# A hybrid decoder step: other transfer times in the order model, and norms spread by a product of 128 rows

## The chip, the cores and the metric

The kernel runs on one core of one Trainium2 chip, in one launch. A time is the device time of that core in microseconds (us). Three executions of the kernel before took 1326.87, 1324.06 and 1327.06 us; their median, 1326.87, is the time before. The profiled execution is a fourth one: 1324.27 us, of which 1322.5 lie between its first and its last instruction (its span).

## The reference, cut to what matters

One layer is computed for 1024 prompt steps and 8 x 8 sample steps, 1088 columns in all, with a model width of 1024:

```
h = rmsnorm(x, g_mix_in)
gate_a, x_a, q, k, v, z_c, xbc, dt_raw = split(h @ w_in)
out_a = rg_lru(conv4(x_a)) * gelu(gate_a)                     # width 256
out_b = three dilated window branches of attention on q, k, v # 6 heads x 64, sample steps with a cache
out_c = rmsnorm(ssd(silu(conv4(xbc)), dt, A) * silu(z_c))     # 6 heads x 64, chunks of 128 steps
x = x + rmsnorm(concat(out_a, out_b, out_c) @ w_out)
x = x + rmsnorm((silu(g) * u) @ w_down)   with  g, u = split(rmsnorm(x) @ w_gate_up)   # width 2816
```

Everything is float32.

## The kernel before, in words

Columns are steps (`T` = 1088), in three groups of 364, 362 and 362 (`GROUPS`). Rows are channels, in tiles of 128. A float32 product is made of three products of rounded parts (`mm3`: high weights by high x, high by low, low by high), so that each weight tile is loaded as float32 from memory, rounded (`round`, on VectorE or ScalarE, whichever the order model finds less loaded) and subtracted (`rest`, on VectorE).

The work has four stretches. First the input is scaled and multiplied by the first two tiles of `w_in`. From about 100 to 640 us TensorE makes the other projections and, from about 415 us, the products of `w_out` (both called main products here; they stand in bank0 and bank6, later in more banks) and between them the three mixers: the chunked scan of mixer C to about 220 us, attention to about 497 us, and then the norms after `w_out`. From 640 to 1220 us it makes the gate, up and down products, and at the end the last tiles and the final norm.

The order of all this is not written out. The generators (`scan`, `unit`, `norm_c`, `out_norm`, `projections` and so on) yield conditions, and class `Flow` keeps a clock of its own, `now`, and a guess for when each engine is free and each piece of memory is written. `Flow.run` takes the first task whose condition holds by that guess; `step` picks for each of the other engines the ready instruction of the lowest rank. What comes out is the order in which instructions are put on each engine, and nothing more: on the chip each engine works through its own list in order, and waits at an instruction whose inputs are not there, with everything behind it. For a transfer on SyncE `step` guesses `QUEUE` for its issue, then `FLIGHT`, then a time by its bytes and `RATE`, one transfer after the other, and then `RECEIPT` until its data count as landed (lines 142, 271 to 274 and 319). `RATE` is in bytes per us.

`inverse_norm` (line 567) turns a sum of squares over 128 partitions into one factor per column, the same on all partitions. A product with ones sums the partitions (128x1, three of them), POOL takes the power, the factors are split into high and low parts, a transpose puts them into 6 rows, VectorE spreads them over a tile `spread` (`t7` in the order) of 6 rows by up to 364 columns with zeros where they don't belong, and one last product, of 6 rows of ones by that tile, puts the factors on all 128 partitions. This runs 14 times: three times for the input, three for mixer C's norm, six after `w_out`, two at the end.

In `chunk` the state `S` of the scan is multiplied by the chunk's decay and gets the chunk's product added, both on VectorE; `y` gets the products with the old state, times `eacb`, a tile that a transfer brings from DRAM. In `attention` each head's q and k come from DRAM (`pd`) by four transfers, and then `unit` makes the scores.

Of the kernel before, what the change touches and what calls it, by code (L numbers as in the profile page):

```python
# [90 lines left out]
def bc(ap, n):  # L91
    return ap[:, :, None].to_broadcast([ap.shape[0], ap.shape[1], n])
# [40 lines left out]
class Flow:  # L133
# [5 lines left out]
    RANKS = {"prep": 0, "norm": 1, "mix": 2, "main": 3}  # L139

    SIGNAL, MARGIN = 0.15, 0.2
    QUEUE, FLIGHT, RECEIPT, RATE = 0.475, 0.65, 0.95, 360e3

    def __init__(self):
        self.now, self.tasks = 0.0, []
# [219 lines left out]
class Trunk:  # L365
# [204 lines left out]
    def inverse_norm(self, ssum, n, lane, spread):  # L570

        nc, F = self.nc, self.flow
        w = ssum.shape[-1]
        yield lambda: F.ok(ssum) and lane.ok() and self.rstd.ok()
        bank = lane.take()
        at = [min(c, w - 128) for c in range(0, w, 128)]
        b = len(at)
        for c, o in enumerate(at):  # L580
            self.mm(bank[:, c:c + 1], ssum[:, o:o + 128], self.k(K_ONE, 1), start=True, stop=True)
        held = self.rstd.take()
        r, both = held[:, 0:b], held[:, 4:4 + 2 * b].rearrange("p (c q) -> p c q", q=2)
        hi, lo = both[:, :, 0], both[:, :, 1]
        with self.prio("prep"):
            nc.vector.tensor_scalar(r, bank[:, :b], 1.0 / n, EPS, op0=ALU.mult, op1=ALU.add)
            nc.gpsimd.tensor_tensor(r, r, self.half[:, :b], op=ALU.pow)
            nc.vector.tensor_copy(hi.bitcast(F32R), r)
            nc.vector.tensor_sub(lo, r, hi)
        yield lambda: F.ok(both) and spread.ok()  # L590
        rows = bank[0:2 * b, 128:256]
        self.tr(rows, held[:, 4:4 + 2 * b], self.k(K_ID))
        whole = spread.take()
        lent, spread, full = spread, whole[0:2 * b, :w], (b - 1) * 128
        with self.prio("prep"):
            nc.vector.tensor_mul(spread[:, :full].rearrange("p (c t) -> p c t", c=b - 1),
                                 rows[:, None, :].to_broadcast([2 * b, b - 1, 128]),
                                 bc(self.k(K_ROW, b - 1)[0:2 * b], 128))
            nc.vector.tensor_scalar(spread[:, full:], rows[:, 128 - (w - full):], self.k(K_ROW + b - 1, 1)[0:2 * b],
                                    None, op0=ALU.mult)  # L600
        self.rstd.give(held)
        yield lambda: F.ok(spread)
        self.mm(bank[:, :w], self.ones[0:2 * b], spread, start=True, stop=True)
        lent.give(whole)
        return bank

# [58 lines left out]
    def setup(self):  # L665
        nc, I = self.nc, self.I
        xr = [self.alloc(T) for _ in range(8)]
        squares = [self.alloc(364) for _ in range(6)]
        sq, ssum = Rot(squares), self.alloc(T)
        self.splits.append(self.pair())  # L670
        with self.prio("prep"):
            nc.vector.memset(self.half, -0.5)
            self.zeros = self.alloc(256)
            nc.vector.memset(self.zeros, 0.0)
            self.warm(2 * WARM)
            nc.scalar.activation(squares[1][:, 0:4], self.half, AF.Square)
            nc.sync.dma_start(self.cols, I["cols"])
            for k in range(KT):
                g = self.col(C_GMI + k)
                for c0, w in GROUPS if k < 4 else [(0, T)]:  # L680
                    sl = slice(c0, c0 + w)
                    nc.sync.dma_start(xr[k][:, sl], I["xT"][k][:, sl])
                    if k == 0 and c0 == 0:
                        self.first_weights(0, 256)
                    nc.scalar.activation(self.XH[:, k, sl], xr[k][:, sl], AF.Copy, scale=g)
                    nc.vector.scalar_tensor_tensor(self.XL[:, k, sl], xr[k][:, sl], g, self.XH[:, k, sl].bitcast(F32),
                                                   op0=ALU.mult, op1=ALU.subtract)
                if k == 1:
                    self.first_weights(256, 1024)
                if k == 4:  # L690
                    self.prep(2)
            nc.sync.dma_start(self.const, I["consts"][:, 0:K_TRI])
            nc.vector.tensor_copy(self.ones, self.k(K_ONE))
            for i in range(2):
                self.pad(self.padded[XA_T + i], I["lru_conv"][i])
            self.pad(self.padded[XBC_T], I["ssd_conv"][0])
            for c0, w in GROUPS:
                sl = slice(c0, c0 + w)
                for k in range(KT):
                    s, x = sq()[:, :w] if k else ssum[:, sl], xr[k][:, sl]  # L700
                    nc.scalar.activation(s, x, AF.Square)
                    if k:
                        nc.vector.tensor_add(ssum[:, sl], ssum[:, sl], s)
        return ssum
# [1379 lines left out]
```

## Time and profile before

| | |
|---|---|
| median of three executions | 1326.87 us |
| profiled execution | 1324.27 us, span 1322.5 |
| TensorE busy, weight loads beside it | 1294.4 us (98%), 1236.8 us |
| VectorE, ScalarE, GpSimd busy | 931.3, 557.1, 46.5 us |
| chain that ended last | TensorE 76%, VectorE 9%, transfers 9% |
| transfers | 179.38 MB, 136 GB/s on average |

In the rows PE is TensorE's products, PEld its weight loads, DVE VectorE, ACT ScalarE, POOL GpSimd, SP SyncE, which issues the transfers. An arrow `<-` after a wait names what ended it. A product's duration is longer than the step to the next one's start, since products overlap.

### The profile page before, as it was taken

Reading aid. Unit: us, or ns where it says so; the run is one execution under the profiler, and the core shown is the slowest. Engines: PE = TensorE matmul, PEld = TensorE weight load, DVE = VectorE, ACT = ScalarE, POOL = GpSimd, SP = SyncE. Lnnn points to the kernel's source line nnn. Section 1 sums busy time; section 2 is a strip of 40 time slices with the busy share of each in tenths; the row PEclk is TensorE's granted clock in tenths of the full one; section 3 lists DMA queues with packets and bytes.
Section 4 is the critical chain, followed back from the end, with each engine's and each line's share of the span. In section 5 each row is a group of like instructions: output and inputs, shape, how many; then the busy total and the mean of one; then the engine's idle time right before and its main releaser. Section 6 shows DMA issues by size and latency. Waiting matters only on the chain.

```text
span 1322.5 us, 22885 instructions
## 1 busy us (share of the span) xinstructions
PE 1294.4 (98%) x8883; PEld 1236.8 (94%) x8883; DVE 931.3 (70%) x1867; ACT 557.1 (42%) x1063; POOL 46.5 (4%) x60
## 2 busy tenths in 40 slices
PE   9999999999999999999999999999999999999997
PEld 8999888899899889989999999999999999999786
DVE  7799795764867977789756666666658856557852
ACT  7364461671675874445222222222223442433312
POOL 0000000000000002420000000000000000000000
PEclk9999999999999999999999999999999999999999
DMA  6122466536737446442132212221023566866651
GB/s 215 29 69 73 125 193 186 166 97 193 215 95 195 142 136 189 159 148 92 46 98 98 78 39 81 98 98 66 34 98 130 174 225 214 301 215 195 193 180 48
DMA packets 92922, 179.38 MB, mean 136 GB/s; under 512 B 15010, under 2 KB 60814, under 8 KB 92814
## 3 DMA queue, kind: packets, MB, share of 16 engines
q1 hardware_dynamic: 92814, 177.93, 43.0%
q8 instruction: 69, 1.13, 0.4%
q14 instruction: 39, 0.32, 0.1%
HBM read 138.61 MB, written 39.28 MB: 135 GB/s over the span
## 4 chain that ended last, share of the span: by engine, by line
PE 76%; DVE 9%; DMA 9%; ACT 2%; issue 2%; SPq 1%; DVEq 0%; POOLq 0%; POOL 0%; ACTq 0%
PE bank L434 74%; DVE t L347 9%; ACT t L347 2%; DMA t<-pd 2%; DMA t<-in_w_in_t 2%; PE bank L438 2%; DMA t<-mixd 2%; SPq L347 1%; DMA t<-yd 1%; DMA t<-eacd 1%; DMA t<-in_w_gu_t 0%; DMA t<-hidd 0%; DMA t<-in_w_out_t 0%; DMA mixd<-t 0%; DMA pd<-t 0%
## 5 line engine op out<-in xcount | busy, mean ns | idle before, releaser
L434 PE MATMUL bank<-t,t 128*128 128x272 f32 (+7 forms) x8505 | 1265.1, 311 | 15.7 <-DVE t L347 12.5
L434 PEld LDWEIGHTS bank<-t,t 128*128 128x128 f32 (+1 forms) x8505 | 1197.7, 186 | 64.5 <-DVE t L347 21.1
L347 DVE TENSOR_TENSOR t<-t,t 128x512 fp32r<-128x512 f32 (+13 forms) x599 | 440.1, 760 | 102.2 <-ACT t L347 93.5
L347 ACT CAST t<-t 128x512 fp32r<-128x512 f32 (+7 forms) x314 | 220.6, 724 | 437.1 <-PE bank L434 178.4
L347 DVE TENSOR_TENSOR t<-t,bank 128x272 f32<-128x272 f32 (+4 forms) x283 | 126.5, 454 | 123.0 <-PE bank L434 122.4
L347 DVE TENSOR_TENSOR t<-bank,t 128x512 fp32r<-128x512 f32 (+11 forms) x227 | 111.7, 511 | 77.1 <-ACT t L347 42.0
L347 ACT ACTIVATE t<-t,t 128x128 f32<-128x128 f32 (+17 forms) x212 | 132.6, 666 | 29.3 <-DVE t L347 13.9
L347 ACT ACTIVATE t<-t 128x272 f32<-128x272 f32 (+9 forms) x173 | 91.5, 537 | 112.7 <-DVE t L347 98.6
L347 POOL TENSOR_TENSOR t<-t,t 128x362 f32<-128x362 f32 (+3 forms) x41 | 43.6, 1077 | 1106.4 <-DVE t L347 1097.6
L347 DVE CAST t<-t 128x1024 fp32r<-128x1024 f32 (+6 forms) x91 | 45.1, 496 | 46.5 <-PE bank L434 34.5
L347 ACT COPY t<-bank 128x272 f32<-128x272 f32 (+7 forms) x122 | 44.5, 373 | 76.9 <-PE bank L434 63.9
L347 DVE TENSOR_TENSOR t<-t 128x272 f32<-128x272 f32 (+8 forms) x147 | 68.2, 465 | 5.3 <-ACT t L347 2.0
L347 DVE SCALAR_TENSOR_TENSOR t<-t,t,t 128x1112 f32<-128x1112 f32 (+6 forms) x68 | 56.9, 861 | 6.0 <-ACT t L347 5.2
L438 PE MATMUL bank<-t,t 128*128 128x128 f32 (+5 forms) x354 | 54.1, 274 | 4.8 <-DVE t L347 3.0
L438 PEld LDWEIGHTS bank<-t,t 128*128 128x128 f32 (+5 forms) x354 | 39.6, 138 | 13.4 <-DVE t L347 7.6
L347 ACT ACTIVATE t<-bank 128x272 f32<-128x272 f32 (+7 forms) x55 | 23.4, 429 | 61.4 <-PE bank L434 60.1
L347 DVE CUSTOM_DVE_ANT_0 t<-bank,t 128x512 f32<-128x512 f32 (+4 forms) x75 | 39.9, 548 | 5.5 <-PE bank L434 5.2
L347 ACT CAST t<-bank 128x512 fp32r<-128x512 f32 (+2 forms) x72 | 35.2, 514 | 19.3 <-PE bank L438 18.9
L347 DVE SCALAR_TENSOR_TENSOR t<-t,t,bank 128x362 f32<-128x362 f32 (+4 forms) x55 | 27.9, 549 | 4.0 <-PE bank L434 2.9
L347 DVE SCALAR_TENSOR_TENSOR t<-t,t 128x1024 f32<-128x1024 f32 (+4 forms) x26 | 20.3, 805 | 2.7 <-ACT t L347 1.5
L347 ACT ACTIVATE t<-bank,t 128x362 f32<-128x362 f32 (+1 forms) x29 | 15.5, 561 | 11.5 <-PE bank L434 11.5
L347 DVE SCALAR_TENSOR_TENSOR t<-t 128x54 f32<-128x54 f32 (+5 forms) x33 | 14.7, 447 | 3.9 <-DMA t<-yd 3.1
(20 smaller groups left out, 76.4 us busy)
## 6 DMA issues: line engine op xcount, KB each, us to landing
t<-in_w_dn SPq DMA_DIRECT2D x66, 512.0 KB, 3.7
t<-in_w_gu_t SPq DMA_DIRECT2D x52, 512.0 KB, 4.5
hidd<-t SPq DMA_DIRECT2D x44, 272.0 KB, 2.1
t<-in_w_in_t SPq DMA_DIRECT2D x21, 512.0 KB, 4.4
t<-hidd SPq DMA_DIRECT2D x44, 176.0 KB, 3.8
t<-in_w_out_t SPq DMA_DIRECT2D x15, 512.0 KB, 3.9
t<-pd SPq DMA_DIRECT2D x24, 256.0 KB, 4.4
t<-in_xT SPq DMA_DIRECT2D x24, 181.0 KB, 3.6
```

Of the source, the lines that this page charges most:

```text
L347: self.flow.note(self.name, what, args, kw, lambda: getattr(self.engine, what)(*args, **kw))
L434: self.flow.product(out, [w, x], start, d, lambda: self.nc.tensor.matmul(out, w, x, **how))
L438: self.flow.product(out, [x], True, d, lambda: self.nc.tensor.transpose(out, x, ident))
```

## The change

The order model is told that transfers are slower: 280,000 instead of 360,000 bytes per us, and 1.25 instead of 0.95 us until they count as landed. The last product of `inverse_norm` reads all 128 rows of the tile `spread` and of the ones. So that the other 122 rows are zero, two copies of 256 columns of zeros are made into that tile at the start (the second begins at column 108).

```diff
@@ class Flow
-    QUEUE, FLIGHT, RECEIPT, RATE = 0.475, 0.65, 0.95, 360e3
+    QUEUE, FLIGHT, RECEIPT, RATE = 0.475, 0.65, 1.25, 280e3
@@ def inverse_norm
         yield lambda: F.ok(spread)
-        self.mm(bank[:, :w], self.ones[0:2 * b], spread, start=True, stop=True)
+        self.mm(bank[:, :w], self.ones, whole[:, :w], start=True, stop=True)
         lent.give(whole)
         return bank
@@ def setup
             nc.vector.tensor_copy(self.ones, self.k(K_ONE))
+            for o in (0, 364 - 256):
+                nc.vector.tensor_copy(self.spread.items[0][:, o:o + 256], self.zeros)
```

The instructions of each engine stay the same but for the two copies (and the engine of some roundings); their order changes from the first norm on. Two places follow.

VectorE in the scan, at about 152 to 158 us before. `t40` is the state S, `t48` holds the decays and step sizes, `t85` is the y of chunk 1 and `t86` its `eacb`, which a transfer brings; the first two rows are two steps of the next chunk's input. Before:

```order
L347 TENSOR_TENSOR t89_1441<-t88_1440,t48_533 128x384
L347 TENSOR_TENSOR t40_525<-t40_525,t48_533 128x384
L347 TENSOR_TENSOR t73_1425<-t73_1425,t77_1429 128x384 x2
L347 TENSOR_TENSOR t85_1437<-bank7_69,t86_1438 128x384
L347 TENSOR_TENSOR t17_100<-bank6_68,t16_99 128x362
L347 TENSOR_TENSOR t40_525<-t40_525,bank2_64 128x384
```

And now:

```order
L347 TENSOR_TENSOR t89_1443<-t88_1442,t48_535 128x384
L347 TENSOR_TENSOR t40_527<-t40_527,t48_535 128x384
L347 TENSOR_TENSOR t40_527<-t40_527,bank2_64 128x384
L347 TENSOR_TENSOR t73_1427<-t73_1427,t77_1431 128x384 x2
L347 TENSOR_TENSOR t17_100<-bank6_68,t16_99 128x362
L347 TENSOR_TENSOR t40_527<-t40_527,t48_535 128x384
L347 TENSOR_TENSOR t85_1439<-bank7_69,t86_1440 128x384
```

The addition to S stood behind the multiplication that reads `t86`, and stands ahead of it now; so does the next multiplication of S.

TensorE at the first head of the last head pair, at about 413 us before. The rows with `t1` and `t2` (the input's parts) are main products, those with `t117` (q), `t118` and `t119` (k) are scores. Before:

```order
L434 MATMUL bank6_68<-t1_73,t13_88 128x362
L434 MATMUL bank0_62<-t1_73,t14_89 128x364
L434 MATMUL bank0_62<-t2_74,t14_89 128x364
L434 MATMUL bank0_62<-t1_73,t15_90 128x364
L434 MATMUL bank2_64<-t118_2142,t117_2141 128x384
L434 MATMUL bank2_64<-t119_2143,t117_2141 128x384
L434 MATMUL bank1_63<-t118_2142,t117_2141 128x512
L434 MATMUL bank1_63<-t119_2143,t117_2141 128x512
```

And now:

```order
L434 MATMUL bank0_62<-t1_73,t15_90 128x364
L434 MATMUL bank6_68<-t1_73,t14_89 128x362
L434 MATMUL bank6_68<-t2_74,t14_89 128x362
L434 MATMUL bank6_68<-t1_73,t15_90 128x362
L434 MATMUL bank2_64<-t118_2160,t117_2159 128x384
L434 MATMUL bank2_64<-t119_2161,t117_2159 128x384
L434 MATMUL bank1_63<-t118_2160,t117_2159 128x512
L434 MATMUL bank1_63<-t119_2161,t117_2159 128x512
```

Before, the scores came after the first 3 main products of the tile in bank0; now they come after all 24 of it and 3 of the tile behind it, 24 main products later. The same scores of the first head pair (at 239 us before) moved 12 main products later. The last product of attention comes in both orders after 1884 of the products of 362 or 364 columns.

## Rows read from the trace of the kernel before

**Rows 1.** The page, busy time, and the chain's share by engine.
```profile
PE 1294.4 (98%) x8883; PEld 1236.8 (94%) x8883; DVE 931.3 (70%) x1867; ACT 557.1 (42%) x1063; POOL 46.5 (4%) x60
...
PE 76%; DVE 9%; DMA 9%; ACT 2%; issue 2%; SPq 1%; DVEq 0%; POOLq 0%; POOL 0%; ACTq 0%
```

**Rows 2.** Windows: stretch, length, busy of PE, PEld, DVE, ACT, POOL, clock, DMA.
```profile
100.00:640.00 540.00, 522.75 (x3575) 488.85 (x3574) 416.54 (x935) 291.51 (x583) 39.19 (x40) 0.99 0.50 150
640.00:1220.00 580.00, 580.00 (x4298) 579.36 (x4297) 374.13 (x666) 180.98 (x333) 0.00 (x0) 1.00 0.39 127
```

**Rows 3.** Waits of PE from 100 to 640 us: total, times, longest.
```profile
PE bank L434 <- DVE t L347: 10.2, 15, 2.1
PE bank L438 <- DVE t L347: 3.0, 4, 1.2
PE bank L434 <- ACT t L347: 2.0, 2, 1.0
PE bank L438 <- DMA t<-pd: 1.0, 1, 1.0
```

**Rows 4.** Groups of PE's products by shape: rows*columns, count, busy, mean ns.
```profile
L434 PE MATMUL bank<-t,t 128*128 128x362 f32 x1512 | 270.7, 331 | 0.5 <-ACT t L347 0.3 <-DVE t L347 0.2
L434 PE MATMUL bank<-t,t 6*128 6x362 f32 x8 | 3.4, 427 | 0.5 <-DVE t L347 0.5
L434 PE MATMUL bank<-t,t 6*128 6x364 f32 x4 | 1.7, 430 | 0.0
L434 PE MATMUL bank<-t,t 6*128 6x352 f32 x2 | 0.8, 422 | 0.0
```

**Rows 5.** Timeline of PE around one product of 6 rows: start, duration.
```profile
541.19 0.33 PE L434 MATMUL bank<-t,t 128*128 128x362 f32 x1
541.45 0.42 PE L434 MATMUL bank<-t,t 6*128 6x362 f32 x1
541.80 0.43 PE L434 MATMUL bank<-t,t 128*128 128x362 f32 x1
542.07 0.33 PE L434 MATMUL bank<-t,t 128*128 128x362 f32 x1
542.24 0.33 PE L434 MATMUL bank<-t,t 128*128 128x362 f32 x1
```

**Rows 6.** Timeline of DVE at the start, with the idle time ahead.
```profile
4.43 0.60 DVE L347 SCALAR_TENSOR_TENSOR t<-t,t,t 128x364 fp32r<-128x364 f32 x1 [3.27 <-ACT t L347]
```

**Rows 7.** Groups of DVE and ACT: rounding of 1024 columns.
```profile
L347 DVE CAST t<-t 128x1024 fp32r<-128x1024 f32 x39 | 27.0, 693 | 35.2 <-PE bank L434 27.9 <-DMA t<-in_w_dn 5.2 <-DMA t<-in_w_out_t 1.4
L347 ACT CAST t<-t 128x1024 fp32r<-128x1024 f32 x83 | 86.7, 1047 | 128.8 <-DMA t<-in_w_dn 45.5 <-DMA t<-in_w_in_t 40.8 <-PE bank L434 20.1
```

**Rows 8.** Timeline of PE: the waits with a late transfer behind them.
```profile
157.65 2.74 PE L434 MATMUL bank<-t,t 128*64 128x128 f32 x28 [1.33 <-DVE t L347]
239.13 1.12 PE L434 MATMUL bank<-t,t 128*128 128x128 f32 x6 [1.11 <-DVE t L347]
333.26 0.98 PE L438 MATMUL bank<-t,t 128*128 128x128 f32 x7 [0.98 <-DMA t<-pd]
413.78 0.41 PE L434 MATMUL bank<-t,t 128*128 128x384 f32 x1 [1.01 <-ACT t L347]
414.95 1.33 PE L434 MATMUL bank<-t,t 128*128 128x384 f32 x3 [0.75 <-DVE t L347]
435.20 1.97 PE L434 MATMUL bank<-t,t 128*128 128x364 f32 x9 [1.02 <-ACT t L347]
467.71 0.55 PE L438 MATMUL bank<-t,t 128*128 128x128 f32 x3 [1.15 <-DVE t L347]
508.92 1.27 PE L434 MATMUL bank<-t,t 128*128 128x1 f32 x8 [2.13 <-DVE t L347]
```

**Rows 9.** The chain in order of time: start, length, transfer.
```profile
149.34 6.71 DMA t<-eacd
...
228.44 7.09 DMA t<-in_w_in_t
...
404.10 7.16 DMA t<-pd
...
500.26 5.04 DMA t<-mixd
```

**Rows 10.** Timeline of DVE in the scan.
```profile
156.14 1.00 DVE L347 TENSOR_TENSOR t<-bank,t 128x384 f32<-128x384 f32 x2 [1.21 <-DMA t<-eacd]
```

**Rows 11.** Windows of PE: length, busy (count), clock, DMA share, GB/s.
```profile
410.00:415.20 5.20, 3.44 (x19) 1.00 0.40 99
415.20:418.70 3.50, 3.50 (x13) 0.51 1.00 258
...
505.00:510.80 5.80, 3.67 (x24) 1.00 0.59 184
510.80:514.30 3.50, 3.50 (x14) 0.51 0.48 152
```

**Rows 12.** Windows as in rows 2, over the second half of attention.
```profile
424.00:440.00 16.00, 14.84 (x93) 13.73 (x92) 14.46 (x37) 13.86 (x31) 0.00 (x0) 1.00 0.56 181
440.00:460.00 20.00, 19.51 (x137) 17.87 (x136) 18.99 (x57) 17.21 (x40) 0.00 (x0) 1.00 0.37 102
...
480.00:497.00 17.00, 16.60 (x109) 15.07 (x108) 12.97 (x27) 12.14 (x23) 0.00 (x0) 1.00 0.16 51
```

## The prediction

> **What bounds the kernel now.** I read the page's busy times and its chain first, then busy time by stretch, then what ended TensorE's waits in the stretch where it has any, and last single instructions around the places that the change touches. TensorE is busy 1294.4 of 1322.5 us and holds 76% of the chain [rows 1]. From 640 to 1220 us it is busy every one of 580 us; from 100 to 640 it is busy 522.75 of 540 [rows 2]. So time can be won in two ways: TensorE's own work gets shorter, or its waits between 100 and 640 us go, and with them what the waits do to its clock. Those waits sum to 10.2 + 3.0 + 2.0 + 1.0 = 16.2 us [rows 3]. The start and the end hold some 10 us more, which the change doesn't touch. The two parts of the change go to the two ways, one each.
>
> **The product of 128 rows.** A product of 6 rows by 362 columns is shown with 427 ns, one of 128 rows by 362 columns with 331 [rows 4]. Products overlap, so the price is read from starts. Around the one at 541.45 us the starts are 541.19 (a main product), 541.45 (the 6 rows), 541.80 and 542.07 (main products) [rows 5]: from the main product ahead to the second one behind, 0.88 us for three products. The undisturbed step is 542.24 - 542.07 = 0.17 us, 0.51 for three. Not only the small product's own step is long (0.35): the step ahead of it is 0.26 and the one behind it 0.27. I read that as a small product that overlaps neither neighbour. So it costs 0.88 - 0.51 = 0.37 us more than a main product of as many columns, and a product of 128 rows by 362 columns is, for TensorE, such a main product: its weights are new, 128 by 128, as those of nearly every main product are. There are 8 + 4 + 2 = 14 [rows 4]: 14 x 0.37 = 5.2 us. All stand among products of 128 rows, in stretches where TensorE has other work to go on with, so the step saved is time saved. The bounds: nothing, if the long steps come from something else at that place (the wait on VectorE just before it, the change of bank); and 5.2 if all of it goes. A loss I exclude: no row has a product of 128 rows and 362 columns dearer than one of 6. I take 5.2, since the two long neighbours can't be explained by the small product's own work.
>
> The Trainium skill speaks against this gain: "TensorE: Matmul & The Clock Gate", section "Why this matters for your kernels", says that a single matmul with a contraction of 32 takes the same time as one of 128, and by that rule this part is worth nothing. The same skill, "TensorEngine Tiling (Array Packing)", section "Key Properties", says that a switch of tiling mode drains the engine, and by that the saving stands; the long steps on both sides in the rows go with the second, and I let the first stand as a rival below.
>
> **The two copies.** They stand in VectorE's order directly behind its first memsets, ahead of the instruction at 4.43 us. VectorE idles 3.27 us there [rows 6]. A rounding of four times as many columns takes 693 ns [rows 7], so both take under 1.4 us in that gap and cost nothing. Without the cover they would delay the first products by those 1.4.
>
> **Roundings that change engine.** VectorE rounded 39 tiles of 1024 columns, in the new order 12; the other 27 go to ScalarE at 1047 instead of 693 ns [rows 7]. Most of them belong to the down products, where TensorE waits for nothing [rows 2], and ScalarE is busy 180.98 of those 580 us. Nothing; 27 x 0.35 = 9.6 us of ScalarE if that cover were gone.
>
> **The order.** The model's transfers are now later, so on every engine an instruction that needs one moves back against those that don't. Nothing is made slower by that as such: the transfers run as before, and each engine still starts an instruction when its inputs are there. Worth it is only what stood behind a transfer later than the model thought. Transfers of some weight in the chain took 5.0 to 7.2 us [rows 9]. For 256 KB, the q and k of a head, the old model gives 0.475 + 0.65 + 0.73 + 0.95 = 2.8 us, the new one 3.3: nearer, and still far below 7.16. Eight waits have such a transfer behind them, in all 1.33 + 1.11 + 0.98 + 1.01 + 0.75 + 1.02 + 1.15 + 2.13 = 9.5 us [rows 8]. Two of these places also cost clock: TensorE was busy 3.44 of the 5.20 us before 415.2 and 3.67 of the 5.80 before 510.8, and then ran 3.4 us at 1.2 instead of 2.4 GHz (0.51 in the window), 13 and 14 products in 3.5 us [rows 11]; half of each 3.4 is lost, 1.7 us. So 9.5 + 3.4 = 12.9 us is the most that the order can win here.
>
> What the new order does at three of them can be read. At 157.65 the product with S waited for VectorE [rows 8], which stood 1.21 us at the multiplication with eacb [rows 10] with the addition to S behind it; that addition now stands ahead. What is late next is y, which TensorE doesn't read. At 239.13 12 main products are put ahead, 12 x 0.17 = 2.0 us against a wait of 1.11. At 413.78 and 414.95 it is 24 products, 4.1 us against 1.01 + 0.75, and without the waits the clock has no cause to fall. These three: 1.33 + 1.11 + 1.76 + 1.7 = 5.9 us. At the other places (333, 435, 468, 509 us) the order changes both ways: the sums for the first norm after w_out have fewer roundings of late weight tiles among them on VectorE, but TensorE's product that reads them comes earlier too. I count nothing there. Against it stand waits that the new order makes. The old order, by the same rules, has 16.2 - 9.5 = 6.7 us of waits with no late transfer behind them [rows 3, 8], and work that is pushed back has to be made up: VectorE is busy 33.5 of 36 us from 424 to 460 [rows 12]. I set 2.4 us against the 5.9, a little over a third of those 6.7, since the later start is the only thing that tightens there. Net 3.5 us; the ends are 12.9 gained, and the loss of the rival below.
>
> **The sum.** 5.2 + 0 + 0 + 3.5 = 8.7 us less: 1324.27 - 8.7 = 1315.6 for an execution like the profiled one. That one lies 2.6 under the median of the runs shown; against the median it is 1326.87 - 8.7 = 1318.2 us, which is the forecast.
>
> **The rivals.**
> - The order wins nothing: new waits take the place of the old ones, and only the product counts. 1326.87 - 5.2 = 1321.7. For it: VectorE's load in [rows 12], and that transfers still land later than the new model thinks [rows 9]. Against it: the reorder at 157 us takes a wait away and puts nothing in its place.
> - The product of 6 rows is no dearer than one of 128, its long steps belong to the place: 1326.87 - 3.5 = 1323.4. Against it: the step behind it, 0.27 us, is a main product's, which waits for nothing [rows 5].
> - Slower: attention falls behind. Its last product stands in both orders at the same count of main products, but the first and the last head pair start 12 and 24 main products later. If VectorE, not TensorE, sets the pace from 424 us on, these 36 x 0.17 = 6.1 us come out as a wait ahead of the first norm after w_out, where main products run short, and the clock falls there twice more, 2 x 1.7. 6.1 + 3.4 = 9.5, with no old wait gone: 1326.87 - 5.2 + 9.5 = 1331.2. It decides from 9.2 us of added waits on. For it: the 33.5 of 36. Against it: TensorE, too, is busy 34.35 of the same 36, and VectorE has 12.97 of 17 us in the last piece before 497, so there is room to make up most of it.
>
> **How the numbers follow.** The forecast 0.56, the order wins nothing 0.24, the product wins nothing 0.12, slower 0.08. A measurement of this kernel tells 0.3% from no change, 4 us: faster is under 1322.9, slower over 1330.9. The forecast's case is nearly all faster (0.53 of 0.56), the second mostly (0.15 of 0.24), the third a third (0.04 of 0.12): faster 0.72; slower 0.07; the rest, 0.21, the same. The range: below, all that the order can win, 1326.87 - 5.2 - 12.9 = 1308.8, taken as 1310 since not every place gains; above, the product without gain and some 2.6 us of spread between executions, 1326.
>
> **What would show it.** The product step: 14 products with 128 rows and none with 6, and steps of 0.17 us on both sides of them. The order: TensorE's waits between 100 and 640 us sum to about 13 us instead of 16, none at the product with S in the scan, and one stretch at half clock fewer. Wrong would be: long steps around the 128-row products as well; waits of over 16 us in that stretch, above all a new one of some us before the first norm after w_out; or a new wait between 640 and 1220 us.

## The result, and the profile after

The changed kernel takes 1308.88 us (median of 4 executions, 1307.71 to 1309.7), the kernel before 1326.96 beside it (1324.06 to 1327.18): ratio 0.9879, 95% interval 0.9861 to 0.9898. By the ratio that is 16 us less, about twice the 8.7 forecast. (The two medians differ by 18.1; in the later rounds of runs the kernel before has medians from 1324.65 to 1325.21, which fits the ratio.) The median lies 1.1 us below the low end of the range; the ratio applied to 1326.87 gives 1310.8, just inside it. The profiled execution took 1307.71 with a span of 1305.9, 16.6 less than the span before. It is the fastest of the four, whose mean granted clocks are 0.999, 0.997, 0.999 and 0.996.

The page of the kernel after, busy times and chain [rows 1]:

```profile
PE 1283.7 (98%) x8883; PEld 1232.6 (94%) x8883; DVE 915.0 (70%) x1839; ACT 583.7 (45%) x1093; POOL 44.6 (3%) x60
...
PE 82%; DVE 8%; DMA 4%; ACT 3%; issue 2%; SPq 1%; DVEq 0%; POOLq 0%; POOL 0%; ACTq 0%
```

The chain lost more than half of its share of transfers, 9 to 4%. Windows of the kernel after: stretch, length, busy time of PE, PEld, DVE, ACT and POOL with counts, granted clock, DMA share, GB/s [rows 2, 11]:

```profile
100.00:640.00 540.00, 528.59 (x3692) 499.87 (x3691) 424.42 (x953) 301.15 (x599) 37.07 (x39) 1.00 0.50 150
640.00:1220.00 580.00, 580.00 (x4255) 576.57 (x4254) 362.99 (x653) 198.00 (x350) 1.71 (x2) 1.00 0.39 128
410.00:415.20 5.20, 5.20 (x35) 5.20 (x34) 5.20 (x12) 2.90 (x6) 0.00 (x0) 1.00 0.94 231
415.20:418.70 3.50, 3.12 (x19) 2.82 (x18) 3.03 (x5) 3.29 (x8) 0.00 (x0) 1.00 0.78 217
```

In the first stretch TensorE now makes 3692 products instead of 3575, in the second it still waits for nothing: the gain lies ahead of 640 us. In this execution the clock no longer falls at 415 us, nor anywhere else from 100 to 1300 us. The first 272-column product of the gate stretch starts at 555.0 instead of 570.7 us, 15.7 of the 16.6 us.

TensorE's waits from 100 to 640 us, total, times, longest [rows 3], and three of the longest (timeline; the brackets hold the wait):

```profile
PE bank L434 <- DVE t L347: 6.4, 8, 1.5
PE bank L438 <- DVE t L347: 4.1, 6, 1.5
...
118.00 0.27 PE L438 MATMUL bank<-t,t 128*54 128x128 f32 x1 [1.54 <-DVE t L347]
...
419.53 0.43 PE L434 MATMUL bank<-t,t 128*128 128x364 f32 x1 [1.21 <-DVE t L347]
...
489.41 0.27 PE L434 MATMUL bank<-t,t 128*128 128x1 f32 x1 [1.46 <-DVE t L347]
```

They sum to 10.5 instead of 16.2. None stands at the scan's S product. The wait at 118.00 has grown: the same instruction waited before, too, for 0.41 us:

```profile
112.97 0.30 PE L438 MATMUL bank<-t,t 128*54 128x128 f32 x1 [0.41 <-DVE t L347]
```

The wait at 419.53 stands at the 1700th of the products of 362 or 364 columns (the spreading ones left out), where VectorE is late; before, the 1702nd waited 1.02 us at 435.20, behind a late transfer [rows 8]. The wait at 489.41 is what is left of the 2.13 at the norm sums [rows 8]. Two more of over 1 us, 1.14 and 1.23 at 554 and 559 us, stand at products that waited 1.13 and 1.23 before.

The products [rows 4], a stretch of them around one that spreads factors (the one at 527.59), the start of VectorE [rows 6], and the roundings [rows 7]:

```profile
L434 PE MATMUL bank<-t,t 128*128 128x362 f32 x1520 | 270.4, 329 | 1.0 <-DVE t L347 0.6 <-ACT t L347 0.3
...
527.09 1.16 PE L434 MATMUL bank<-t,t 128*128 128x362 f32 x6
...
1.20 0.62 DVE L347 CAST t<-t 128x256 fp32r<-128x256 f32 x2
4.39 0.60 DVE L347 SCALAR_TENSOR_TENSOR t<-t,t,t 128x364 fp32r<-128x364 f32 x1 [2.56 <-ACT t L347]
...
L347 ACT CAST t<-t 128x1024 fp32r<-128x1024 f32 x110 | 115.1, 1047 | 121.3 <-DMA t<-in_w_dn 57.8 <-DMA t<-in_w_in_t 23.3 <-PE bank L434 19.2
L347 DVE CAST t<-t 128x1024 fp32r<-128x1024 f32 x12 | 8.3, 689 | 0.9 <-DMA t<-in_w_dn 0.5 <-PE bank L434 0.4
```

The 8 products of 6 by 362 are now among the 1520 of 128 by 362. Six products in 1.16 us are five steps of 0.166 and one duration of 0.33: the spreading product leaves no mark. That is so at 11 of the 14. The other three (48.21, 496.56, 560.49 us) wait for VectorE just then: a step of 0.25 to 0.57 ahead and an own step of 0.27 stay. These save about 0.2 us each: at 48.46 us before, the three steps are 0.57, 0.36 and 0.27, at 48.21 now 0.57, 0.27 and 0.17. The two copies lie in VectorE's gap, and the instruction behind them starts at 4.39 instead of 4.43.

What the prediction looked at in one place only [rows 10] is VectorE's own waits for transfers. Of the kernel before, then of the kernel after, from 100 to 640 us:

```profile
DVE t L347 <- DMA t<-in_w_in_t: 3.5, 1, 3.5
DVE t L347 <- DMA t<-yd: 3.1, 2, 1.7
DVE t L347 <- DMA t<-in_w_out_t: 1.4, 3, 0.5
DVE t L347 <- DMA t<-hd: 1.3, 1, 1.3
DVE t L347 <- DMA t<-eacd: 1.2, 1, 1.2
```

```profile
DVE t L347 <- DMA t<-in_ssd_state: 1.1, 1, 1.1
DVE t L347 <- DMA t<-eacd: 0.5, 1, 0.5
DVE t L347 <- DMA t<-yd: 0.4, 1, 0.4
```

With the smaller ones they sum to 12.2 before and 2.0 after.

### The profile page after: what moved, and what is told of

Its sections match the earlier page's. It is cut to its first block, busy times and chain, and to the rows that moved or that the text cites. A ratio compares the mean times of both kernels' runs of the same rounds, so it can differ in the third digit from the quotient of the medians.

```text
span 1305.9 us, 22830 instructions
## 1 busy us (share of the span) xinstructions
PE 1283.7 (98%) x8883; PEld 1232.6 (94%) x8883; DVE 915.0 (70%) x1839; ACT 583.7 (45%) x1093; POOL 44.6 (3%) x60
## 3 DMA queue, kind: packets, MB, share of 16 engines
q8 instruction: 69, 1.13, 0.4%
## 4 chain that ended last, share of the span: by engine, by line
PE 82%; DVE 8%; DMA 4%; ACT 3%; issue 2%; SPq 1%; DVEq 0%; POOLq 0%; POOL 0%; ACTq 0%
PE bank L434 80%; DVE t L347 8%; ACT t L347 3%; PE bank L438 2%; DMA t<-pd 1%; SPq L347 1%; DMA t<-eacd 1%; DMA t<-in_w_in_t 0%; DMA t<-in_w_out_t 0%; DMA pd<-t 0%; DMA t<-acd 0%; DMA out_vT<-t 0%; DMA t<-mixd 0%; ACT L347 0%; DVEq L2072 0%
## 5 line engine op out<-in xcount | busy, mean ns | idle before, releaser
L434 PE MATMUL bank<-t,t 128*128 128x272 f32 (+9 forms) x8505 | 1255.8, 311 | 10.0 <-DVE t L347 8.3
L434 PEld LDWEIGHTS bank<-t,t 128*128 128x128 f32 (+2 forms) x8505 | 1194.2, 185 | 52.8 <-DVE t L347 17.6
L347 DVE TENSOR_TENSOR t<-t,t 128x512 fp32r<-128x512 f32 (+12 forms) x599 | 443.4, 762 | 129.1 <-ACT t L347 122.7
L347 ACT CAST t<-t 128x512 fp32r<-128x512 f32 (+7 forms) x344 | 249.2, 748 | 385.3 <-PE bank L434 158.4
L347 DVE TENSOR_TENSOR t<-bank,t 64x256 f32<-64x256 f32 (+12 forms) x227 | 112.5, 512 | 81.2 <-ACT t L347 46.6
L347 ACT COPY t<-bank 128x272 f32<-128x272 f32 (+8 forms) x122 | 44.4, 372 | 84.9 <-PE bank L434 72.5
L347 DVE SCALAR_TENSOR_TENSOR t<-t,t,t 128x1112 f32<-128x1112 f32 (+7 forms) x68 | 56.9, 861 | 5.1 <-ACT t L347 4.1
L347 DVE CAST t<-t 128x512 fp32r<-128x512 f32 (+8 forms) x63 | 26.0, 412 | 14.4 <-PE bank L434 6.9
L347 DVE SCALAR_TENSOR_TENSOR t<-t,t 128x1024 f32<-128x1024 f32 (+4 forms) x26 | 20.3, 804 | 1.4 <-ACT t L347 1.4
```

Source lines behind the costliest of these rows:

```text
L347: self.flow.note(self.name, what, args, kw, lambda: getattr(self.engine, what)(*args, **kw))
L434: self.flow.product(out, [w, x], start, d, lambda: self.nc.tensor.matmul(out, w, x, **how))
```

## The experiments

**The product alone.** The order model keeps its old numbers; the zeros come from GpSimd so that VectorE's list stays as it was.

```
-        self.mm(bank[:, :w], self.ones[0:2 * b], spread, start=True, stop=True)
+        self.mm(bank[:, :w], self.ones, whole[:, :w], start=True, stop=True)
...
+        self.tc.nc.gpsimd.memset(self.spread.items[0].bitcast(F32), 0.0)
```

> The order and its constants as before, the last product of each norm with 128 rows; the zeros come from one memset on GpSimd at the start, so that no other instruction moves. Theory (a product of 6 rows overlaps neither neighbour, 0.37 us each, 14 times): 5.2 us faster than before, ratio 0.996; steps of 0.17 us around the products; TensorE's waits between 100 and 640 us still 16 to 17 us and both stretches at half clock still there. Rival (the long steps belong to the place): no change, ratio 1.000, long steps stay. Second rival (the product carries most of the whole gain, since the shorter norm chain lets later work come earlier): over 8 us, ratio under 0.994.

Measured: 1320.7, ratio 0.9975 [0.9957, 0.9993], so 3.3 us less, between 0.9 and 5.7. The steps are plain at 11 of 14 products; the other three wait for VectorE. TensorE's waits sum to 17.6 us, a little over the 16 to 17 expected. Of the two stretches at half clock only one is left, though the order is that of before. Before, TensorE was busy 3.67 of the 5.80 us before 510.8 and then ran at 0.51 [rows 11]. Here (windows as above) it is busy 3.71 of the same 5.80 us, with a wait of 2.09 instead of 2.13 in them, and keeps its clock:

```profile
505.00:510.80 5.80, 3.71 (x25) 3.42 (x24) 4.41 (x9) 3.07 (x6) 1.26 (x1) 1.00 0.52 178
510.80:514.30 3.50, 3.50 (x24) 3.42 (x23) 3.36 (x8) 0.93 (x2) 0.71 (x1) 1.00 0.43 152
```

So whether a wait also costs clock is not settled by the order alone.

**The order alone.** The changed kernel, with the product of 6 rows again; on every engine the order is that of the changed kernel.

```
-        self.mm(bank[:, :w], self.ones, whole[:, :w], start=True, stop=True)
+        self.mm(bank[:, :w], self.ones[0:2 * b], spread, start=True, stop=True)
```

> The changed kernel with the last product of each norm back at 6 rows; its order is that of the changed kernel on every engine. Theory (the two parts add; the order took 5.8 us of TensorE's waits and two stretches at half clock, 3.4 us, and some 2 us of smaller stalls): 16.6 - 5.2 = 11.4 us faster than before, ratio 0.9914, and about 5 us slower than the changed kernel. Rival (the order wins only the waits that can be seen, and the rest is the product's): 6 us faster, ratio 0.9955.

Measured: 1312.83, ratio 0.9913 [0.9896, 0.993]: 11.5 us less. 0.9975 x 0.9913 = 0.9888 against the 0.9879 of both: within their intervals the parts add. The profiled execution has two stretches at half clock that the one of the changed kernel, in the same order, doesn't have (windows as above, the stretch ahead of each and the stretch itself). Over all executions the two kernels differ less: the granted clock is 0.996 to 0.999 in the six here and in the four there.

```profile
417.00:422.40 5.40, 4.12 (x24) 3.34 (x23) 5.27 (x14) 3.88 (x10) 0.00 (x0) 1.00 0.89 271
422.40:425.90 3.50, 3.50 (x14) 3.50 (x13) 3.04 (x8) 3.05 (x7) 0.00 (x0) 0.52 1.02 335
553.00:558.90 5.90, 4.77 (x30) 3.98 (x29) 3.60 (x10) 1.03 (x3) 0.00 (x0) 1.00 0.19 52
558.90:562.40 3.50, 3.50 (x19) 3.45 (x17) 3.50 (x9) 2.51 (x3) 0.86 (x1) 0.51 0.15 47
```

**How many rows it takes.** The order before; the 14 products get row counts from 6 to 128 in turn; rows 6 to 127 hold zeros.

```
+        n_rows = next(self.row_counts)
+        self.mm(bank[:, :w], self.ones[0:n_rows], whole[0:n_rows, :w], start=True, stop=True)
...
+        self.row_counts = iter([6, 32, 33, 64, 65, 96, 97, 112, 120, 127, 128, 128, 64, 128])
```

> The order of before; the 14 last products of the norms have 6, 32, 33, 64, 65, 96, 97, 112, 120, 127, 128, 128, 64, 128 rows, in that order of time (the rows beyond 6 are zero, so the result stays the same). Theory (what counts is whether the array is used in another tile shape than by the neighbours: 32 or 64 rows): long steps of 0.26, 0.35 and 0.27 us at 6, 32, 33 and 64 rows, steps of 0.17 from 65 rows on. Rival (any product with fewer rows than its neighbours is long): long up to 127 rows. Rival (only the smallest shape is long): long at 6 and 32, short from 33 on.

Measured, in one execution: groups by shape (rows*columns, count, busy time, mean ns):

```profile
L434 PE MATMUL bank<-t,t 6*128 6x364 f32 x1 | 0.4, 431 | 0.0
L434 PE MATMUL bank<-t,t 32*128 32x362 f32 x1 | 0.4, 428 | 0.0
L434 PE MATMUL bank<-t,t 64*128 64x364 f32 x1 | 0.4, 428 | 0.0
...
L434 PE MATMUL bank<-t,t 127*128 127x362 f32 x1 | 0.3, 334 | 0.0
...
L434 PE MATMUL bank<-t,t 65*128 65x362 f32 x1 | 0.3, 329 | 0.0
...
L434 PE MATMUL bank<-t,t 96*128 96x362 f32 x1 | 0.3, 328 | 0.0
```

The steps from start to start agree (ns; step ahead, own step, step behind): 6 rows 259, 361, 269; 32 rows 253, 358, 280; 64 rows 259, 357, 270; 65 rows 165, 165, 171; 96 rows 164, 166, 171; 127 rows 162, 173, 170. Between 64 and 65 rows the whole extra time goes, some 0.39 us, at products that stand in the same surroundings. The second product of 64 rows, with 352 columns, is long as well (327, 353, 338), and so is that of 33; those of 97, 112 and 120 rows are short. So it is not the place, and not the work in the rows, but 64 rows or fewer between products of more. The Trainium skill, "TensorE: Matmul & The Clock Gate", section "Why this matters for your kernels", gives one product of 32 rows the time of one of 128; here the 32 rows cost 253 + 358 + 280 ns for three steps where 65 rows cost 501. "TensorEngine Tiling (Array Packing)", section "Key Properties", lets a switch of mode drain the engine; the long steps on both sides agree with that. No run here shows whether such a switch is the cause.

**The model's transfers later still.** Everything of the change, and the numbers moved as far again.

```
-    QUEUE, FLIGHT, RECEIPT, RATE = 0.475, 0.65, 1.25, 280e3
+    QUEUE, FLIGHT, RECEIPT, RATE = 0.475, 0.65, 1.6, 220e3
```

> The changed kernel with RATE 220e3 and RECEIPT 1.6: transfers land still later in the order model (256 KB after 3.9 us, 512 KB after 5.1, where the profile of before has medians of 4.4 and 4.4). Theory (the nearer the model is to the transfers, the fewer waits): TensorE's waits between 100 and 640 us fall from 10.5 to about 8 us, 2 to 3 us faster than the changed kernel. Rival (each order is a draw among orders): within 5 us of the changed kernel on either side, the waits stand at other places, not fewer. Rival (mixers pushed back too far, so that main products run short at the end of attention): 3 us or more slower, with a wait of over 3 us before the first norm after w_out.

Measured: 1327.14, ratio 1.0021 [1.0005, 1.0036]: all of the gain is gone again, where the theory had 2 to 3 us more of it. From 100 to 640 us TensorE waits 10.4 us, not the 8 expected. But the gate stretch starts at 551.1, 3.9 us earlier than in the changed kernel, so the loss does not lie where the slower rival put it, ahead of the first norm after `w_out`. Most of it is at one place in the down products. Timeline of TensorE, of ScalarE (with waits), and SyncE's issues ahead of it:

```profile
1143.96 0.96 PE L434 MATMUL bank<-t,t 128*128 128x352 f32 x2 [9.19 <-ACT t L347]
```

```profile
1142.87 1.43 ACT L347 CAST t<-t 128x1024 fp32r<-128x1024 f32 x2 [12.62 <-DMA t<-in_w_dn]
```

```profile
1124.35 5.83 SPq L347 DMA_DIRECT2D t<-x1d  x3
1130.28 3.59 SPq L347 DMA_DIRECT2D t<-in_w_dn  x1
```

The three loads of the residual `x1d` (1408, 1408 and 1536 KB) are put ahead of a tile of `w_down`, which is rounded 12.6 us after it is issued. TensorE waits 9.2 us; its clock falls 4.5 us before the wait ends and stays at 0.50 for 10.2 us. Together that is 9.2 + (10.2 - 4.5) / 2 = 12 us. Some more goes at two other stretches at half clock (windows as above):

```profile
562.60:566.10 3.50, 3.50 (x17) 3.50 (x17) 3.50 (x7) 1.01 (x2) 3.23 (x3) 0.51 0.15 52
613.80:620.70 6.90, 5.70 (x23) 5.39 (x24) 6.35 (x8) 2.46 (x4) 0.00 (x0) 0.51 0.21 85
```

In the changed kernel a tile of `w_down` goes out first, and TensorE is busy throughout while the loads run:

```profile
1116.00:1126.00 10.00, 10.00 (x64) 10.00 (x63) 7.24 (x12) 5.71 (x11) 0.00 (x0) 1.00 1.06 374
```

**The same, with the changed numbers from the second half on.** One line more, at the start of `second_half`, that is from the products of `w_out` for the second group on:

```
+        F.RECEIPT, F.RATE = 1.25, 280e3
```

> As the kernel with RATE 220e3 and RECEIPT 1.6, but from the start of the second half on (the products of w_out for the second group) the order model has the changed kernel's 280e3 and 1.25 again. Theory (its loss is one place: the three loads of the residual, 4.3 MB, stand on SyncE ahead of a tile of w_down, which then lands 12.6 us after its issue and leaves TensorE 9.2 us without work and then at half clock): without that place it keeps what it won before 551 us, 3.9 us against the changed kernel: 1303 to 1306, ratio to before 0.985. Rival (each order is a draw, the second half's too): 1306 to 1320, with another wait of over 2 us after 640 us.

Measured: 1307.08, ratio 0.9857 [0.9826, 0.9889]. That is 1 us above the theory's range, and the rival's new wait didn't come: there are 0.2 us of waits between 640 and 1220 us. But the line changes the order from about 488 us on, and so more than that place. Of the 20.1 us between the two spans the place at 1143 us makes some 12, TensorE's waits before 640 us make 3.4 (10.4 against 7.0), and less time at half clock elsewhere some 3. So the place is the largest part of the loss of 1327.14, not all of it. With it gone, the later model does as well as the changed one, within the intervals.

**One number at a time, and between.** The changed kernel with only the receipt changed (1.25, 360e3), only the rate (0.95, 280e3), and both a little more (1.4, 250e3):

```
-    QUEUE, FLIGHT, RECEIPT, RATE = 0.475, 0.65, 1.25, 280e3
+    QUEUE, FLIGHT, RECEIPT, RATE = 0.475, 0.65, 1.25, 360e3
...
+    QUEUE, FLIGHT, RECEIPT, RATE = 0.475, 0.65, 0.95, 280e3
...
+    QUEUE, FLIGHT, RECEIPT, RATE = 0.475, 0.65, 1.4, 250e3
```

> The changed kernel with RATE 360e3 as before and RECEIPT 1.25. Theory (later landing in the model takes waits away in step with how much later it is; a transfer of 256 KB is 0.3 of the 0.5 us later, one of 64 KB nearly all): TensorE's waits from 100 to 640 us between 13 and 15 us, time between 1311 and 1318 (ratio about 0.991). Rival (each order is a draw): anywhere from 1305 to 1322, waits from 8 to 18 us with no relation to the constants.

> The changed kernel with RECEIPT 0.95 as before and RATE 280e3. Theory (in step with how much later): 512 KB are 0.42 us later, 64 KB nearly nothing; waits from 100 to 640 us between 13 and 16 us, 1312 to 1319. Rival (a draw): anywhere from 1305 to 1322.

> The changed kernel with RATE 250e3 and RECEIPT 1.4, between the changed one and the still later one. Theory (in step): waits from 100 to 640 us about 11 us, the first product of the gate stretch starts between 551 and 555 us, and if w_down's tile stays ahead of the residual's loads, 1303 to 1309. Rival (a draw): start of the gate stretch anywhere from 550 to 567 us, total 1303 to 1325.

Measured: receipt only 1322.22, ratio 0.9972 [0.9954, 0.999], no better than the product alone and above the theory's 1311 to 1318; rate only 1305.43, ratio 0.9844 [0.9818, 0.9871], the fastest kernel of all, below the 1312 to 1319 of the theory and with 7.3 us of waits instead of 13 to 16; between 1307.98, ratio 0.9864 [0.9837, 0.9891], within the 1303 to 1309, though its gate stretch starts at 549.8, earlier than the 551 to 555. "In step with how much later" fails: net, the receipt wins nothing and the rate all. With the receipt alone VectorE still waits 12.0 us for transfers from 100 to 640 us; with the rate alone 1.8:

```profile
DVE t L347 <- DMA t<-in_w_in_t: 1.3, 1, 1.3
DVE t L347 <- DMA t<-eacd: 0.5, 1, 0.5
```

With the receipt alone TensorE waits 15.7 us against 17.6 with the product alone, but its profiled execution falls to half clock four times and loses more there. Two of the four (windows: the stretch ahead, then the stretch at half clock):

```profile
225.00:230.60 5.60, 3.20 (x20) 2.89 (x18) 0.54 (x1) 0.00 (x0) 0.00 (x0) 1.00 0.87 239
230.60:234.10 3.50, 3.09 (x13) 3.09 (x14) 1.01 (x2) 1.94 (x5) 0.00 (x0) 0.52 0.18 63
318.00:322.70 4.70, 2.75 (x18) 2.46 (x16) 2.88 (x5) 2.04 (x2) 0.00 (x0) 1.00 0.62 239
322.70:329.60 6.90, 6.83 (x25) 6.68 (x26) 2.64 (x7) 0.00 (x0) 0.85 (x1) 0.51 0.29 85
```

**A row of rates.** Receipt 0.95, product of 128 rows, the rate 320e3, 250e3, 220e3 and 180e3 up to `second_half`, and 0.95 and 280e3 from there on, so that the down products don't mix in.

```
-    QUEUE, FLIGHT, RECEIPT, RATE = 0.475, 0.65, 1.25, 280e3
+    QUEUE, FLIGHT, RECEIPT, RATE = 0.475, 0.65, 0.95, 320e3
...
+        F.RECEIPT, F.RATE = 0.95, 280e3
```

> The changed kernel with 0.95 us and 320 KB/ms*1000 (320e3) for the model up to the start of the feed-forward part, 0.95 and 280e3 from there on; 280e3 all through gave 1305.4, 360e3 with the product of 128 rows 1320.7. Theory (the rate decides, by VectorE's waits for transfers, 1.8 us at 280e3 and about 10 at 360e3 between 100 and 640 us): in between, VectorE waits 3 to 8 us for transfers there, 1309 to 1317 us. Rival (each order is a draw, the times have no order by the rate): anything from 1304 to 1322, with waits for transfers that don't go with the time.

> The same with 0.95 and 250e3 up to the feed-forward part, then 0.95 and 280e3. Theory: VectorE's waits for transfers between 100 and 640 us are gone already at 280e3 (1.8 us), so under 2 us and the same time as at 280e3 within a few us, 1301 to 1307. Rival (a draw): as likely over 1308 as under.

> The same with 0.95 and 220e3 up to the feed-forward part, then 0.95 and 280e3. Theory: VectorE waits under 2 us for transfers between 100 and 640 us, 1301 to 1309: nothing is left to win by a lower rate, and little is lost. If the loss at 220e3 and 1.6 us (1327.1) came from the stretch before the feed-forward part after all, over 1312. Rival (a draw): as likely over 1308 as under.

> The same with 0.95 and 180e3 up to the feed-forward part, then 0.95 and 280e3: the model's transfers now land later than most real ones do. Theory: VectorE waits under 2 us for transfers, but work that could run is pushed back and TensorE waits for it: 1306 to 1318 us. Rival (a draw): no worse than 220e3 or 250e3, 1302 to 1310.

Measured, with the other kernels beside them. "VectorE" is its waits for transfers, "TensorE" its waits, both from 100 to 640 us; "half" is TensorE's time at half clock from 100 to 1300 us; "rest" is the span less TensorE's waits and half of "half" (and less 9.8 us of waits behind 640 us in the kernel with 1.6 and 220e3). All but time and ratio are of the profiled execution. The rounds have kernels before of 1324.65 to 1326.96 us beside them, so ratios compare better than times.

| receipt, rate | product | time, ratio [interval] | VectorE | TensorE | half | span | rest |
|---|---|---|---|---|---|---|---|
| 0.95, 360e3 (before) | 6 rows | 1326.96 | 12.2 | 16.2 | 6.8 | 1322.5 | 1302.9 |
| 1.25, 280e3 | 6 rows | 1312.83, 0.9913 [0.9896, 0.993] | 2.4 | 8.6 | 6.8 | 1310.7 | 1298.7 |
| 0.95, 360e3 | 128 | 1320.7, 0.9975 [0.9957, 0.9993] | 14.0 | 17.6 | 3.4 | 1317.8 | 1298.5 |
| 1.25, 360e3 | 128 | 1322.22, 0.9972 [0.9954, 0.999] | 12.0 | 15.7 | 23.9 | 1322.4 | 1294.8 |
| 0.95, 320e3 | 128 | 1318.0, 0.9954 [0.9929, 0.9979] | 9.3 | 14.0 | 10.2 | 1315.3 | 1296.2 |
| 0.95, 280e3 | 128 | 1305.43, 0.9844 [0.9818, 0.9871] | 1.8 | 7.3 | 3.4 | 1303.4 | 1294.4 |
| 1.25, 280e3 (after) | 128 | 1308.88, 0.9879 [0.9861, 0.9898] | 2.0 | 10.5 | 0 | 1305.9 | 1295.4 |
| 0.95, 250e3 | 128 | 1313.1, 0.9906 [0.9883, 0.9928] | 2.3 | 11.3 | 13.7 | 1312.4 | 1294.3 |
| 1.4, 250e3 | 128 | 1307.98, 0.9864 [0.9837, 0.9891] | 0.9 | 9.1 | 6.8 | 1307.3 | 1294.8 |
| 0.95, 220e3 | 128 | 1309.36, 0.9879 [0.986, 0.9899] | 0 | 7.3 | 6.8 | 1308.1 | 1297.4 |
| 1.6, 220e3, then 1.25, 280e3 | 128 | 1307.08, 0.9857 [0.9826, 0.9889] | 0.9 | 7.0 | 3.4 | 1305.0 | 1296.3 |
| 1.6, 220e3 | 128 | 1327.14, 1.0021 [1.0005, 1.0036] | 1.3 | 10.4 | 20.5 | 1325.1 | 1294.7 |
| 0.95, 180e3 | 128 | 1325.76, 1.0014 [1.0001, 1.0028] | 2.3 | 20.3 | 17.1 | 1323.5 | 1294.7 |

Two things follow. First, the rest is 1294.3 to 1298.5 in all eleven kernels with the product of 128 rows: TensorE's waits and its time at half clock account for a spread of 22 us to within 2 us either way. (Half clock inside a wait, up to 5.9 us, is in both; counted once, and with all waits behind 640 us, the rest is 1293.9 to 1298.4.) That says where the time is, and not what put it there. Secondly, there is a trend by the rate, and a scatter on it. From 360e3 to 280e3 VectorE's waits for transfers fall from 14.0 over 9.3 to 1.8, and the time with them; below, they stay low, and at 180e3 work is pushed back so far that TensorE waits 20.3 us, by now for VectorE and ScalarE alone. The transfers' own speed is of that size: in the windows above where their share is 0.87 to 1.06 they move 231 to 374 GB/s. The trend is not the clock's: with (1 - granted clock) x span taken off each execution, an estimate of what the clock costs, the medians of the spans are 1314.5 at 360e3, 1309.6 at 320e3, 1301.0 at 280e3, 1304.8 at 250e3, 1303.9 at 220e3 and 1313.0 at 180e3. The expectations had the trend, but not its size at the ends: 320e3 is 1 us above its range, 220e3 0.4 and 180e3 8 us. The scatter is what the expectation for 250e3 missed: 1313.1, where 1301 to 1307 was expected of the rate. VectorE waits no more for transfers there, but TensorE waits 11.3 us instead of 7.3, and in the profiled execution, the slowest of four, it runs 13.7 us instead of 3.4 at half clock, in three places, two of them here:

```profile
418.00:423.60 5.60, 3.35 (x19) 2.39 (x18) 5.60 (x18) 4.25 (x12) 0.00 (x0) 1.00 0.76 278
423.60:430.50 6.90, 5.49 (x29) 4.04 (x30) 5.83 (x17) 4.36 (x10) 0.00 (x0) 0.51 0.04 11
476.90:481.70 4.80, 2.64 (x15) 2.04 (x14) 1.66 (x3) 1.46 (x3) 0.00 (x0) 0.99 0.52 148
481.70:485.10 3.40, 3.40 (x13) 3.40 (x12) 1.72 (x3) 0.44 (x1) 0.00 (x0) 0.51 0.70 182
```

So neither theory holds alone: the rate decides between some 1320 and some 1308 us, and 4 to 8 us more go by where waits are left and by whether the clock falls there. The second is in part luck of the execution: by the estimate above, the four executions of the changed kernel lose 1.3 to 5.2 us to the clock. That the profiled one has no stretch at half clock, and the one with the same order and the small product two, is of this kind.

What goes with the rate was sought on ScalarE as well. Its waits for transfers from 100 to 640 us don't go with the time: 69.1 us before, 53.2 in the changed kernel and 51.7 in the fastest, but 37.0 with the receipt alone and 27.8 at 180e3. VectorE's do down to 280e3, though not one by one: the kernel with the row counts, in the order of before, has 8.6 us of them and the product alone 14.0, in spans of 1318.6 and 1317.8. The longest, 3.5 us at 220 us, is missing from the first, and in neither does TensorE wait near it.

## Why the prediction was right, and where its size was off

**The product (5.2): right in mechanism, a little large.** Measured alone 3.3 [0.9, 5.7]; on top of the new order (0.9879 against 0.9913) 4.5. Eleven of 14 saved their 0.37, 4.1 us; three keep long steps and save about 0.2 each, because VectorE is late there, so "TensorE has other work to go on with" failed at those three. The rival that the product wins nothing falls with the step between 64 and 65 rows.

**The copies and the roundings (0 and 0): right.** The copies lie in the gap; 12 roundings stay on VectorE and 110 stand on ScalarE, as forecast, and TensorE is busy all of 640 to 1220 us.

**The order (3.5 net): right in kind, a third of its size.** This is the step that failed: 11.5 us were measured alone and 12.7 on top of the product (0.9879 against 0.9975), each to within about 2.5. What the profiled executions show of it, before against after: waits 16.2 - 10.5 = 5.7, half clock 6.8 / 2 = 3.4, and the rest 1298.5 (product alone) - 1295.4 = 3.1, in all 12.2 us. Against the sum in the prediction:

1. The waits. The three places that were read won their 4.2 us, as forecast. Of the four counted at nothing, those at 333, 468 and 509 us won 0.98 + 1.15 + 0.67 = 2.8; at 435 us a wait of 1.21 has taken the place of the 1.02. All other waits were charged with 2.4 us; they grew from 6.7 to 7.8, by 1.1. So the waits fell to 10.5 instead of the 13 forecast.
2. The clock. One stretch at half clock was counted as going; in the profiled execution both went. In part that is luck: the product alone, in the old order, lost one of them too. Over all executions the size is about right: the median granted clock is 0.995 in 50 executions of the kernel before and 0.998 in the four after, by the estimate 6.6 and 2.6 us.
3. The rest. These 3.1 us, steps inside what the windows call busy, were in no term. Added up by shape from start to start, against the product alone and without waits and half clock, they are spread: products of 364 columns take 1.6 us less in all, the mixers' products of 128 and 384 columns and their smallest ones 3.0 less, those of 362 and 256 columns 1.7 more. What makes these steps shorter is not shown.

The bound of 12.9 for the order held, but in part by luck: it was made of 9.5 us of waits and 3.4 of clock, and 3.1 of what was measured are in neither. Cutting it by more than two thirds because not every place gains was not sound. The low end was worked out as 1308.8 and then raised to 1310 by the same argument; that the time is 1308.88 is a coincidence.

**What the view missed.** The argument took eight places one by one and followed each back to a transfer. What goes with the time from 360e3 to 280e3 stands on VectorE, not on TensorE: 12.2 us in which VectorE stands at an instruction whose transfer has not landed, with everything behind it queued. The change takes ten of these away at once, and down to 280e3 the time falls with them. That is a trend over orders: no run takes one of these waits away alone, so that they are the cause is argued and not shown. Of the two numbers only the rate does it; the receipt time alone gives 1322.22 against the 1320.7 of the product alone.

**The slower rival** (attention falls behind VectorE) didn't come at these numbers. Something like it shows at 180e3: 20.3 us of waits for VectorE and ScalarE, 17.1 us at half clock between 388 and 416 us, and the gate stretch starts at 572.4. But most of these waits stand inside attention, not ahead of the first norm after `w_out`, where the rival had them.

## What to carry to other kernels

Where an order is made by a model, first sum the waits for transfers on every engine that feeds the busy one. Here the time followed VectorE's sum until that was near nothing: one number that brought the model's transfers near the speed of the real ones was worth more than the places found one by one, and one too slow lost it again. Two settings that are equal by that sum can still differ by several us, by the waits that are left and by whether the clock falls, which the same order does in one execution and not in another. So try a few settings, read the clock of every execution, and look at the span less waits and half clock before explaining a difference. A product of 64 rows or fewer between products of 128 was worth widening with zeros to more than 64 rows here.

## What was not expected of the hardware

Products of 6, 32 and 64 rows among products of 128 all cost about 0.39 us more than one of 65 (with 6 rows, steps of 259, 361, 269 against 165, 165, 171 ns), with a sharp edge between 64 and 65 rows. A spreading product of 128 rows that has to wait for VectorE still has an own step of 0.27 us, where the others have 0.165 (three of 14 each in the changed kernel and with the product alone). And almost the same stretch, 3.67 or 3.71 of 5.80 us busy, was followed by half clock in one execution and by full clock in another.
